# The tokens' scale goes into the halves of x at the end of k, and five evictions lose it

## The chip, the cores and the metric

The kernel runs on one core of a Trainium2 chip. A core has TensorE (PE in the profile, with its weight loads shown apart as PEld), VectorE (DVE), ScalarE (ACT), GpSimd (POOL) and SyncE (SP), which issues nearly all DMAs here. The engines run side by side, each through its own list of instructions, and wait for one another by semaphores. The metric is the time of one execution on the device in microseconds (us), the median of several runs.

## What is computed

Two transformer-like blocks follow each other on 256 tokens of width 1024. The change is in the first one, in how it uses its normalised input `h`:

```python
def first_block(x, ...):
    h = rms_norm(x, norm_w[layer])              # y = x * rsqrt(mean(x*x) + EPS), times norm_w
    proj = h @ w_in[layer].astype(f32)          # 1024 -> all widths
    u_s, z_s, q, k, v, z_a, r_s, r_a = jnp.split(proj, offsets, axis=-1)
    y_s = s5_branch(u_s, ...)                   # state-space branch
    y_s = (y_s * jax.nn.silu(z_s)) @ w_ssm_out[layer].astype(f32)
    q = rms_norm(q...); k = rms_norm(k...)      # per head, then rotary embedding
    y_a = dilated_attention(q, k, v)
    y_a = (y_a * jax.nn.silu(z_a)) @ w_attn_out[layer].astype(f32)
    m = jax.nn.sigmoid(r_s) * y_s + jax.nn.sigmoid(r_a) * y_a
    x = (x.astype(f32) + m @ w_o[layer].astype(f32)).astype(x.dtype)
```

The second block (a gated recurrence, a differential attention, and 32 experts of which each token uses two) is not touched.

## The kernel before

**Scale after the product.** `norm_w` belongs to a column of `h`, the factor `rsqrt(mean)` to a token. The kernel multiplies x by `norm_w` alone (`raw`, L1093), keeps the result as `hr` (f32, 8 pieces of 128 rows by 256 tokens), and starts on the products with `w_in` before the token's factor is known. The factor exists in two forms: `self.rstd`, one number for each partition when tokens lie on partitions, and `self.rows`, all 256 factors in a row on every partition. Each eviction of a product from PSUM multiplies by one of the two.

**Products.** The first block's products come in the order u, k, v, q, za, ra, zs, rs, glu, ao, so, wo. For u and k (`WHOLE`) the f32 operands are multiplied whole (`dense`, L453). For all others both operands are split into a rounded high half on ACT and a low half, the difference, on DVE (`split`, L597), and three products are summed: `dense` again (L453), or `dense_wide` (L477) for v and q. The halves of x are `hT[0]` and `hT[1]`, buffers in the pool R. They are made by `halves(c)`, c = 0 to 3, two of the eight pieces each, from `hr`, and put into a list (`self.mid`) from which `dense` takes a step after every few products of k's last chunk.

**Evictions.** `heads` (k) and `heads2` (q) copy a product out of PSUM on ACT with `rstd`, square it on ACT into a temporary of the small heap E, and add the squares by head on DVE (L1189, L1200). v is copied out on ACT with `rstd`. The gates z and r use `rows`: `scaled` multiplies PSUM by `rows` on DVE, then ACT takes the tanh of the result, and for z (`silu2`) DVE multiplies once more. E holds three temporaries of 128 x 512 at a time, and hands out the one that has been free longest.

**Work beside the products.** The state-space branch runs as a generator (`ssm`, L699), four rounds of 16 groups each: DVE prepares tables, PE makes transposes and small products (L764, L779), DVE turns the states (a scan, L801), and writes them to `hst[0]` and `hst[1]` (L807, L811), which PE reads next (L833, L836). Head normalisation, attention and the splits of the weights (`WR<-WR`, L253 and L272) are woven in as well.

**Order.** The Python code gives an order of the whole. A scheduling layer then places every instruction in its engine's list by what it depends on and by what that layer reckons things take; the lists are fixed in the built program. At run time an engine goes through its list from the front.

**The end.** The experts' weights stream in over the second half. They are issued by SP when buffers come free, so the start of this stream hangs on the products before it.

Of the kernel before, what the change touches and what calls it, by code (L numbers as in the profile page):

```python
# [12 lines left out]
AF = mybir.ActivationFunctionType  # L13
ALU = mybir.AluOpType
# [208 lines left out]
def shaped(ap, shape):  # L223
    if len(shape) == 1:
        return ap
    names = "abcdef"[:len(shape)]
    kw = {n: s for n, s in zip(names[1:], shape[1:])}
    return ap.rearrange(f"p ({' '.join(names)}) -> p {' '.join(names)}", **kw)
# [12 lines left out]
class Kernel:  # L241
# [803 lines left out]
    def first_block(self):  # L1045
# [31 lines left out]
        hr = self.WR.alloc(8, 256, dt=F32)  # L1077
# [29 lines left out]
        hT = []  # L1107

        def halves(c):
            def f():  # L1110
                w = slice(2 * c, 2 * c + 2)
                self.split(hT[0][:, w], hT[1][:, w], hr[:, w])
                if c == 3:
                    hr.free()
            return f
# [36 lines left out]
        for c in range(4):  # L1152
            ev = evac_to(uT)(c)

            def evac(ps, c=c, ev=ev):
                ev(ps)
                nc.sync.dma_start(ud[:, 2 * c:2 * c + 2], uT[:, 2 * c:2 * c + 2])

            if c:
                self.dense("u", hr, None, evac)  # L1160
            else:
                self.dense("u", hr, None, lambda ps, evac=evac: self.mid.extend(
                    [norm, lambda: None, self.token_rows, lambda: evac(ps)]), rows_first=True)
            if c == 1:
                next(tables)
# [17 lines left out]
        def heads(c, raw, sq):  # L1183
            def g(ps):
                self.scaled_tok(raw[:, 2 * c:2 * c + 2].rearrange("p m t d -> p t m d"),
                                ps.rearrange("p t (m d) -> p t m d", m=2))
                t = self.E.alloc(2, 2, 128)
                self.act(t.ap, raw[:, 2 * c:2 * c + 2], AF.Square)
                V.tensor_reduce(out=shaped(sq, (12, 2, 2))[:, 2 * c:2 * c + 2], in_=t.ap.rearrange("p m t (h d) -> p m t h d", d=64),  # L1189
                                axis=AX, op=ALU.add)  # L1190
                t.free()
            return g

        def heads2(c, raw, sq):
            def g(ps, tb):
                w = raw[:, 4 * c:4 * c + 4, tb]
                self.act(w, ps.rearrange("p (m d) -> p m d", m=4), AF.Copy, scale=self.rstd[:, tb:tb + 1])
                t = self.E.alloc(4, 128)
                self.act(t.ap, w, AF.Square)
                V.tensor_reduce(out=shaped(sq, (12, 2, 2))[:, 4 * c:4 * c + 4, tb],  # L1200
                                in_=t.ap.rearrange("p m (h d) -> p m h d", d=64), axis=AX, op=ALU.add)
                t.free()
            return g
# [6 lines left out]

        def silu2(dst, c):
            def g(ps):
                self.silu2(dst[:, 2 * c:2 * c + 2], ps)
            return g

        def tanh_half(dst, c):
            def g(ps):
                self.tanh_half(dst[:, 2 * c:2 * c + 2], ps)
            return g

        def last(which, c):

            if which == WHOLE[-1] and c == 5:
                hT.extend((R.alloc(8, 256), R.alloc(8, 256)))
                self.mid.extend(halves(i) for i in range(4))

        def operand(which):
            return (hr, None) if which in WHOLE else hT

        att = None  # L1230
        for which in ORDER[1:ORDER.index("so")]:
            if which not in WHOLE:
                ssm_side[1] = SIDE[6]
            if which in ("k", "q"):
                raw = big[which]
                raw.ap = shaped(raw.ap, (12, 2, 128))
                sq = self.sq[which]
                if which in WHOLE:
                    for c in range(6):
                        last(which, c)  # L1240
                        self.dense(which, *operand(which), heads(c, raw, sq), token_major=True)
                else:
                    for c in range(3):
                        self.dense_wide(which, *hT, heads2(c, raw, sq))
                preps[which] = self.head_prep(which, raw.ap, sq)
                self.side_add(preps[which], SIDE[1])
                trans[which] = raw
            elif which == "v":
                v = big["v"]
                v.ap = shaped(v.ap, (2, 24, 64))  # L1250
                for c in range(3):
                    def ev(ps, tb, c=c):
                        self.act(v[:, tb, c * 8:c * 8 + 8], ps.rearrange("p (h d) -> p h d", d=64), AF.Copy,
                                 scale=self.rstd[:, tb:tb + 1])
                    self.dense_wide("v", *hT, ev)
            elif which in width:
                g = gate[which] = F.alloc(width[which], 256)
                for c in range(width[which] // 2):
                    self.dense(which, hT[0], hT[1], (silu2 if which[0] == "z" else tanh_half)(g, c))
                if which == LAST_H:  # L1260
                    for b in (*hT, self.rows):
                        b.free()
                    self.rows = None
            elif which == "mask":
                self.amask = F.alloc(1024)
                nc.sync.dma_start(self.amask.ap, I["amask"])
            elif which == "att":
                for n in "qk":
                    self.side_drain(preps[n])
                for n in "qk":  # L1270
                    self.show(n + "T", trans[n].ap.rearrange("p m t d -> p m (t d)"))
                ao = F.alloc(4, 256)
                att = self.attention(trans["q"], trans["k"], v, gate["za"], ao)
                self.side_add(att, SIDE[2])
            elif which == "ssm":
                self.side_drain(ssm)
                for b in self.m3 + self.bbp + [self.bd, self.d0, self.stab] + self.ptab + self.hst + [u2, uT]:
                    b.free()
                self.show("y2", self.g_hi.ap.bitcast(F32))
            elif which == "attend":  # L1280
                self.side_drain(att)
                for b in (trans["q"], trans["k"], v, gate["za"], self.amask):
                    b.free()
                self.show("att", ao.ap)
            elif which == "ao":
                a_hi, a_lo = R.alloc(4, 256), R.alloc(4, 256)
                for hp in range(4):
                    self.split(a_hi[:, hp], a_lo[:, hp], ao[:, hp])
                ao.free()
                ra = gate["ra"]  # L1290
                for c in range(4):
                    def ev(ps, c=c):
                        w = slice(2 * c, 2 * c + 2)
                        self.stt(ra[:, w], ra[:, w], 1.0, ps, ALU.add, ALU.mult)
                    self.dense("ao", a_hi, a_lo, ev, k=4)
                a_hi.free()
                a_lo.free()
            elif which == "glu":
                zs = gate["zs"]
                s_hi, s_lo = R.alloc(8, 256), R.alloc(8, 256)  # L1300
                for c in range(4):
                    def ev(ps, c=c):
                        w = slice(2 * c, 2 * c + 2)
                        t, y = self.E.alloc(2, 256), self.E.alloc(2, 256)
                        self.act(t.ap, ps, AF.Tanh, scale=0.25)
                        self.add(y.ap, self.g_hi[:, w].bitcast(F32), self.g_lo[:, w].bitcast(F32))
                        self.stt(t.ap, t.ap, 1.0, y.ap, ALU.add, ALU.mult)
                        self.mul(t.ap, t.ap, zs[:, w])
                        self.split(s_hi[:, w], s_lo[:, w], t.ap)
                        t.free()  # L1310
                        y.free()
                    self.dense("glu", self.g_hi, self.g_lo, ev)
                self.g_hi.free()
                self.g_lo.free()
                zs.free()
# [1003 lines left out]
```

## Time and profile before

| what | before |
|---|---|
| median of 3 runs (lowest, highest) | 1038.18 us (1036.95, 1039.09) |
| the profiled execution, its own time | 1038.15 us |
| its span, first to last instruction | 1036.4 us |
| busy share PE / DVE / ACT / POOL | 90% / 50% / 34% / 1% |
| mean granted TensorE clock | 0.974 of full speed |

Busy time counts an engine from the start to the end of each instruction. Matmuls overlap each other, so a busy PE has not necessarily a full pace. Times in rows are microseconds from the start of the span; the trace is of one execution.

### The profile page before, as it was taken

Reading aid. Unit: us, or ns where it says so; the run is one execution under the profiler, and the core shown is the slowest. Engines: PE = TensorE matmul, PEld = TensorE weight load, DVE = VectorE, ACT = ScalarE, POOL = GpSimd, SP = SyncE. Lnnn points to the kernel's source line nnn. Section 1 sums busy time; section 2 is a strip of 40 time slices with the busy share of each in tenths; the row PEclk is TensorE's granted clock in tenths of the full one; section 3 lists DMA queues with packets and bytes.
Section 4 is the critical chain, followed back from the end, with each engine's and each line's share of the span. In section 5 each row is a group of like instructions: output and inputs, shape, how many; then the busy total and the mean of one; then the engine's idle time right before and its main releaser. Section 6 shows DMA issues by size and latency. Waiting matters only on the chain.

```text
span 1036.4 us, 16567 instructions
## 1 busy us (share of the span) xinstructions
PE 932.3 (90%) x6723; PEld 644.8 (62%) x6723; DVE 521.0 (50%) x1166; ACT 352.1 (34%) x586; POOL 11.6 (1%) x39
## 2 busy tenths in 40 slices
PE   9999999999999999999999999877868787776875
PEld 6877788998999988888999844221313132131312
DVE  8998988887767778596768521110101010010101
ACT  3237567565564456554654311000000000000000
POOL 2000000000000000000000000000000000000000
PEclk9999999999999999998999999989999898998989
DMA  7754454555447765652569899999999999999996
GB/s 253 221 171 140 145 163 144 169 180 177 149 129 239 229 216 164 197 181 89 184 197 333 328 391 421 421 421 421 421 421 421 421 421 421 421 420 421 421 417 255
DMA packets 61459, 294.24 MB, mean 284 GB/s; under 512 B 10944, under 2 KB 13376, under 8 KB 37824
## 3 DMA queue, kind: packets, MB, share of 16 engines
q1 hardware_dynamic: 61376, 293.11, 75.5%
q8 instruction: 55, 0.90, 0.4%
q14 instruction: 28, 0.23, 0.1%
HBM read 290.98 MB, written 2.10 MB: 283 GB/s over the span
## 4 chain that ended last, share of the span: by engine, by line
PE 54%; DMA 37%; DVE 6%; ACT 2%; issue 1%; POOL 0%; SPq 0%; DVEq 0%; ACTq 0%
PE d L453 27%; DMA heap<-in_w_dram 23%; PE d L477 12%; DMA WR<-in_w_dram 12%; DVE heap L253 3%; PE h L1982 2%; DMA WR<-in_w_last_dram 2%; DVE WR L253 1%; ACT heap L272 1%; PE d L502 1%; PE s L925 1%; PE r L2014 1%; PE o L959 1%; PE s L944 1%; PE d L1804 1%
## 5 line engine op out<-in xcount | busy, mean ns | idle before, releaser
L453 PE MATMUL d<-R,WR 128*128 128x256 f32 x1920 | 240.5, 285 | 0.4 <-DVE WR L253 0.3
L453 PEld LDWEIGHTS d<-R,WR 128*128 128x128 f32 x1920 | 232.8, 192 | 5.2 <-issue 2.6
L1982 PE MATMUL h<-heap 128*32 128x512 f32 x1024 | 179.3, 675 | 61.0 <-DMA heap<-in_w_dram 60.1
L253 DVE TENSOR_TENSOR WR<-WR,WR 128x1024 fp32r<-128x1024 f32 x140 | 171.1, 1223 | 72.4 <-PE d L453 20.7
L272 ACT ACTIVATE WR<-WR 128x1024 fp32r<-128x1024 f32 x140 | 148.2, 1058 | 126.3 <-PE d L453 77.3
L1982 PEld LDWEIGHTS h<-heap 128*32 128x32 f32 x1024 | 40.4, 121 | 185.5 <-DMA heap<-in_w_dram 110.0
L477 PE MATMUL d<-WR,R 128*128 128x512 f32 x624 | 149.5, 396 | 1.9 <-DVE WR L253 1.0
L477 PEld LDWEIGHTS d<-WR,R 128*128 128x128 f32 x624 | 116.1, 189 | 27.7 <-ACT heap L272 1.7
L253 DVE TENSOR_TENSOR heap<-heap 128x512 f32<-128x512 f32 (+7 forms) x250 | 109.4, 493 | 1.1 <-ACT heap L272 0.4
L272 ACT ACTIVATE heap<-heap 128x512 f32<-128x512 f32 (+5 forms) x133 | 68.8, 531 | 60.6 <-DVE heap L253 28.5
L2014 PE MATMUL r<-WR,heap 128*32 128x512 f32 (+1 forms) x288 | 79.3, 550 | 10.8 <-DMA WR<-in_w_dram 9.9
L269 DVE SCALAR_TENSOR_TENSOR WR<-r,ring,WR 128x512 fp32r<-128x512 f32 (+1 forms) x18 | 12.4, 692 | 135.4 <-ACT WR L272 135.4
L2014 PE MATMUL r<-R,heap 128*32 128x512 f32 (+1 forms) x288 | 69.8, 551 | 9.0 <-ACT heap L272 4.8
L453 PE MATMUL d<-WR,WR 128*128 128x256 f32 x320 | 73.1, 388 | 1.1 <-ACT heap L272 1.1
L453 PEld LDWEIGHTS d<-WR,WR 128*128 128x128 f32 x320 | 61.5, 194 | 11.5 <-ACT heap L272 2.6
L253 DVE TENSOR_TENSOR heap<-heap,h 128x512 f32<-128x512 f32 x8 | 5.5, 687 | 117.3 <-PE h L1982 117.2
L2014 PEld LDWEIGHTS r<-WR,heap 128*32 128x32 f32 x288 | 19.0, 109 | 56.5 <-DMA WR<-in_w_dram 27.0
L272 ACT ACTIVATE WR<-r,ring 128x512 fp32r<-128x512 f32 (+1 forms) x18 | 11.5, 640 | 123.9 <-PE r L2014 112.2
L272 ACT ACTIVATE heap<-h,ring 128x512 f32<-128x512 f32 x8 | 5.5, 687 | 141.3 <-PE h L1982 119.7
L269 DVE SCALAR_TENSOR_TENSOR heap<-heap,h 128x512 f32<-128x512 f32 x8 | 5.5, 687 | 90.3 <-ACT heap L272 90.3
L2014 PEld LDWEIGHTS r<-R,heap 128*32 128x32 f32 x288 | 14.6, 109 | 36.0 <-issue 15.5
L272 ACT ACTIVATE heap<-r 128x512 f32<-128x512 f32 x8 | 4.8, 597 | 82.4 <-PE r L1997 82.4
(211 smaller groups left out, 798.6 us busy)
## 6 DMA issues: line engine op xcount, KB each, us to landing
heap<-in_w_dram SPq DMA_DIRECT2D x128, 1024.0 KB, 19.8
WR<-in_w_in_dram SPq DMA_DIRECT2D x114, 512.0 KB, 4.0
R<-in_w_dram SPq DMA_DIRECT2D x28, 1024.0 KB, 19.8
WR<-in_w_dram SPq DMA_DIRECT2D x28, 1024.0 KB, 19.8
WR<-in_w_wo_dram SPq DMA_DIRECT2D x16, 512.0 KB, 5.9
WR<-in_w_glu_dram SPq DMA_DIRECT2D x8, 512.0 KB, 4.1
WR<-in_w_so_dram SPq DMA_DIRECT2D x8, 512.0 KB, 4.6
R<-in_w_last_dram SPq DMA_DIRECT2D x8, 512.0 KB, 12.6
```

The costliest lines, as they stand in the source:

```text
L253: (eng or self.V).tensor_tensor(out=out, in0=a, in1=b, op=op)
L269: self.V.scalar_tensor_tensor(out=out, in0=a, scalar=s, in1=b, op0=op0, op1=op1)
L272: self.A.activation(out, a, func, **kw)
L453: self.PE.matmul(ps[:, j], lhsT, rhs, start=h == 0 and i == 0 and n == 0, stop=h == k - 4 and kk == 3 and n == len(terms) - 1, skip_group_ ...
L477: self.PE.matmul(ps[tb], x[:, h + kk, sl], w[:, kk], start=h == 0 and kk == 0 and n == 0, stop=h == 6 and kk == 1 and n == 2)
L502: self.PE.matmul(ps[c][:, j], lhsT, rhs, start=h == 0 and i == 0 and n == 0, stop=h == 4 and kk == 3 and n == 2, skip_group_check=True)
L925: PE.matmul(ps[hh][:, cols], qT[r, q, qs], kT[r, q, k], start=True, stop=True)
L944: PE.transpose(pt[:, kb], s[:, kb * 128:(kb + 1) * 128], self.ident)
L959: PE.matmul(po[hp][r, qb], v[:, tb, g * 8 + hp * 2 + hh], ts_[hh][:, kb], start=kb == 0, stop=kb == 3)
L1804: PE.matmul(ps, x[:, 4 * h + kk, tb * 128:tb * 128 + 128], ws[h][w][:, kk], start=h == 0 and kk == 0 and n == 0, stop=h == 1 and kk == 3 a ...
L1982: PE.matmul(ph[sl[g]], xg[:, kk, sl[g]], w(name, kk // 4, g)[:, kk % 4], start=kk == 0, stop=kk == 7)
L2014: PE.matmul(pys[c][sl[g]], hT[:, kk, sl[g]], rhs, start=kk == 0, stop=kk == 3)
```

## The change

The scale moves from the evictions to the operand. `halves(c)` first multiplies its two pieces of `hr` by `rows` on DVE, into a temporary of E, and splits that instead of `hr`. So `hT` holds the halves of the finished `h`, and every product that reads `hT` comes out scaled. The evictions of q, v, za, ra, zs and rs lose the factor: the ACT copies of q and v keep their place without `rstd`; for the four gates the DVE multiplication falls away, ACT takes the tanh from PSUM directly, and the last DVE operation of `silu2` reads PSUM too. u and k keep their scaling, since they multiply `hr`. The second block keeps its own.

```diff
         def halves(c):
             def f():
                 w = slice(2 * c, 2 * c + 2)
-                self.split(hT[0][:, w], hT[1][:, w], hr[:, w])
+                t = self.E.alloc(2, 256)
+                self.scaled(t.ap, hr[:, w])
+                self.split(hT[0][:, w], hT[1][:, w], t.ap)
+                t.free()
                 if c == 3:
                     hr.free()
...
-                self.act(w, ps.rearrange("p (m d) -> p m d", m=4), AF.Copy, scale=self.rstd[:, tb:tb + 1])
+                self.act(w, ps.rearrange("p (m d) -> p m d", m=4), AF.Copy)
...
         def silu2(dst, c):
             def g(ps):
-                self.silu2(dst[:, 2 * c:2 * c + 2], ps)
+                t = self.E.alloc(2, 256)
+                self.act(t.ap, ps, AF.Tanh, scale=0.5)
+                self.stt(dst[:, 2 * c:2 * c + 2], t.ap, 1.0, ps, ALU.add, ALU.mult)
+                t.free()
...
         def tanh_half(dst, c):
             def g(ps):
-                self.tanh_half(dst[:, 2 * c:2 * c + 2], ps)
+                self.act(dst[:, 2 * c:2 * c + 2], ps, AF.Tanh, scale=0.5)
```

The order in PE's list stays the same up to the attention's transposes, but DVE's and ACT's lists change. The first place is ACT's list at the start of the program, where x arrives (`WR<-heap,prm` is a piece of `hr`, `heap<-heap` the square for the mean, `R<-WR` the high half of x):

```order
 L272 ACTIVATE ring<-ones 128x1
 L272 ACTIVATE WR_64<-heap,prm 128x256
 L272 ACTIVATE heap<-heap 128x512
-L272 ACTIVATE R_61<-WR_64 128x512
 L272 ACTIVATE WR_64<-heap,prm 128x256
 L272 ACTIVATE heap<-heap 128x512
-L272 ACTIVATE R_61<-WR_64 128x512
```

All four high halves, and on DVE the four subtractions for the low ones, leave the first 14 us. They come back in the second place, during the products of k. On ACT, the rows ahead are the copies of the first round's block matrix from PSUM (`heap<-s`) and eight small copies for the second round (`64x8x16`), the rows behind k's next eviction (`d,rstd`):

```order
 L272 ACTIVATE heap<-s 32x8x32 x4
 L272 ACTIVATE heap<-heap 64x8x16 x8
+L272 ACTIVATE R_61<-heap 128x512 x2
 L272 ACTIVATE heap<-d,rstd_210 128x2x128 x2
 L272 ACTIVATE heap<-heap 128x8x63
 L272 ACTIVATE heap<-heap 128x512
 L272 ACTIVATE WR_67<-WR_63 128x1024
-L272 ACTIVATE WR_851<-WR_97 128x1024
+L272 ACTIVATE R_61<-heap 128x512
```

Two of the four high halves now stand behind those eight copies, one behind the next split of weights, and the fourth further down. The third place is DVE's list at the same time. Before, the sums of k's squares (L1189) are followed by the second round's preparation and by the first round's states, which DVE takes from PSUM (`s_515`):

```order
L253 TENSOR_TENSOR heap<-heap 128x512 x13
L1189 TENSOR_REDUCE heap<-heap 128x8
L253 TENSOR_TENSOR heap<-heap 128x512 x2
L253 TENSOR_TENSOR heap<-heap 128x2x32 x2
L266 TENSOR_SCALAR heap<-heap 128x2x32
L1189 TENSOR_REDUCE heap<-heap 128x8
L253 TENSOR_TENSOR heap<-heap 128x512 x2
L253 TENSOR_TENSOR heap<-s_515,heap 128x2x4x64 x2
```

Now the same line stands three lines lower in the file (L1192), and two whole splits stand between the third sum and the first round's states:

```order
L253 TENSOR_TENSOR heap<-heap 128x512 x12
L1192 TENSOR_REDUCE heap<-heap 128x8 x2
L253 TENSOR_TENSOR heap<-WR_64,heap 128x512
L253 TENSOR_TENSOR R_62<-heap,R_61 128x512
L253 TENSOR_TENSOR heap<-WR_64,heap 128x512
L253 TENSOR_TENSOR R_62<-heap,R_61 128x512
L253 TENSOR_TENSOR heap<-heap 128x512 x2
L253 TENSOR_TENSOR heap<-s_515,heap 128x2x4x64 x2
```

Each split is a multiplication by `rows` into the temporary, and a subtraction that needs ACT's high half of it. The two are `halves(0)` and `halves(3)`. Both were given the same piece of E (that of the third k chunk's squares), so the second multiplication overwrites what the first subtraction reads, and comes after it. `halves(1)` and `halves(2)` stand 20 to 40 instructions further down. Behind these rows DVE's list is the same up to the writing of `hst[0]`.

## Rows read from the trace of the kernel before

**Rows 1.** Cores: span and mean granted clock.

```profile
core 0: 1036.4 us, clock 0.974
```

**Rows 2.** Stretches: length, busy time by engine, granted clock, DMA share, GB/s.

```profile
core 0: us, PE busy (x) PEld busy (x) DVE busy (x) ACT busy (x) POOL busy (x), PEclk, DMA share, GB/s
60.00:92.50 32.50, 29.63 (x385) 25.31 (x377) 27.16 (x44) 16.48 (x36) 0.00 (x0) 1.00 0.39 129
92.50:122.00 29.50, 28.69 (x275) 23.02 (x273) 29.46 (x55) 20.27 (x38) 0.00 (x0) 1.00 0.50 149
...
177.00:328.00 151.00, 150.15 (x1473) 142.83 (x1471) 120.10 (x248) 86.35 (x137) 1.08 (x2) 1.00 0.51 167
328.00:545.00 217.00, 215.85 (x1506) 195.10 (x1505) 160.31 (x296) 118.58 (x178) 0.53 (x1) 0.98 0.58 186
545.00:606.00 61.00, 60.26 (x428) 52.11 (x427) 37.23 (x88) 21.91 (x39) 3.38 (x15) 1.00 0.90 337
606.00:1036.00 430.00, 335.40 (x1934) 113.32 (x1932) 45.93 (x132) 32.13 (x64) 0.00 (x0) 0.95 0.99 410
```

**Rows 3.** Chain that ended last, where it passes from PE to DMA: start, length, what.

```profile
642.89 2.81 PE h L1982 x24
...
645.71 20.95 DMA WR<-in_w_dram
```

**Rows 4.** Waits of PE, 0 to 400 us: us in total, times, longest.

```profile
PE s L833 <- DVE heap L253: 1.8, 1, 1.8
...
PE s L779 <- ACT heap L272: 1.1, 2, 0.6
PE d L477 <- ACT heap L272: 0.9, 1, 0.9
```

**Rows 5.** Timeline of PE, 58 to 82 us: start, length, idle time before.

```profile
61.33 9.33 PE L453 MATMUL d<-WR,WR 128*128 128x256 f32 x42
72.45 0.43 PE L833 MATMUL s<-heap 128*32 128x64 f32 x16 [1.79 <-DVE heap L253]
72.81 2.86 PE L453 MATMUL d<-WR,WR 128*128 128x256 f32 x12
```

**Rows 6.** Timeline of DVE, 56 to 76 us.

```profile
60.75 0.69 DVE L1189 TENSOR_REDUCE heap<-heap 128x8 f32<-128x512 f32 x1 [2.41 <-ACT heap L272]
61.35 1.41 DVE L253 TENSOR_TENSOR heap<-heap 128x512 f32<-128x512 f32 x2
62.68 1.28 DVE L253 TENSOR_TENSOR heap<-s,heap 128x512 f32<-128x512 f32 x2
```

**Rows 7.** Timeline of ACT, 58.5 to 73 us.

```profile
62.16 2.31 ACT L272 ACTIVATE heap<-heap 64x128 f32<-64x128 f32 x8
68.54 0.84 ACT L272 ACTIVATE heap<-d,rstd 128x256 f32<-128x256 f32 x2 [4.06 <-PE d L453]
```

**Rows 8.** Halves of x, 5 to 15 us: ns least/median/most, first and last start.

```profile
L272 ACT ACTIVATE R<-WR x4: 614/614/614, 6.2 to 12.2; 128x512 fp32r<-128x512 f32 x4
L253 DVE TENSOR_TENSOR R<-WR,R x4: 683/684/687, 7.4 to 13.5; 128x512 fp32r<-128x512 f32 x4
```

**Rows 9.** Groups by form, 177 to 332 us, a split of activations: busy, mean ns, idle before.

```profile
L253 DVE TENSOR_TENSOR R<-heap,R 128x512 fp32r<-128x512 f32 x4 | 2.8, 692 | 2.8 <-ACT R L272 2.8
...
L272 ACT ACTIVATE R<-heap 128x512 fp32r<-128x512 f32 x4 | 2.5, 631 | 2.7 <-DVE heap L253 2.7
```

**Rows 10.** Groups by form, 177 to 332 us, the gates' multiplications by `rows`.

```profile
L253 DVE TENSOR_TENSOR heap<-d,heap 128x512 f32<-128x512 f32 x14 | 9.6, 684 | 0.0
```

**Rows 11.** Timeline of PE, 855 to 885 us, an expert's products around a wait.

```profile
856.77 3.63 PE L1982 MATMUL h<-heap 128*32 128x512 f32 x30
...
865.92 6.01 PE L1982 MATMUL h<-heap 128*32 128x512 f32 x30 [0.73 <-DMA heap<-in_w_dram]
```

**Rows 12.** Stretches behind that wait, columns as in Rows 2.

```profile
866.00:870.00 4.00, 4.00 (x20) 0.92 (x24) 0.00 (x0) 0.00 (x0) 0.00 (x0) 0.50 1.01 420
870.00:873.00 3.00, 1.93 (x14) 0.44 (x6) 0.46 (x1) 0.69 (x1) 0.00 (x0) 0.92 1.02 426
```

More of the change, by code (lines that the diff above doesn't have):

```diff
@@ L1252, in ev @@
                     def ev(ps, tb, c=c):
-                        self.act(v[:, tb, c * 8:c * 8 + 8], ps.rearrange("p (h d) -> p h d", d=64), AF.Copy,
-                                 scale=self.rstd[:, tb:tb + 1])
+                        self.act(v[:, tb, c * 8:c * 8 + 8], ps.rearrange("p (h d) -> p h d", d=64), AF.Copy)
                     self.dense_wide("v", *hT, ev)
```

## Prediction

> **What bounds the kernel now.** I read the cores first: one core, span 1036.4 us, clock 0.974 [rows 1]. The profiled execution took 1038.15 us, 1.75 us more than its span, and the median of the runs is 1038.18, so sums made against this execution need no correction. Next the stretches [rows 2]. PE is full wherever the change acts: it idles 2.87 us between 60 and 92.5 (the end of k), 0.81 in the first part of v up to 122, 0.85 in the gates and ra, rs (177 to 328), 1.15 in the rest of the block. DVE is full only between 92.5 and 122 (29.46 of 29.50 us); in the gates it has 31 us to spare. From 606 us on DMA is full (0.99) and PE is not: there the weights' stream sets the time. The chain that ended last [rows 3] says what the stream's start hangs on: back to 645.71 us it is DMA, and ahead of that it is PE. So whatever PE loses in the first block starts the stream later, and the end moves by as much; whatever PE wins is won to the end. The waits of PE [rows 4] then give the places where the first block loses time at all. The longest is 1.8 us, at the first reading of `hst[0]` (L833), for DVE.
>
> The timeline of PE shows that place [rows 5]: k's last products run from 61.33 to 70.66, PE idles 1.79, reads `hst[0]` at 72.45, and behind that stand k's last twelve products. DVE's timeline shows what makes it late [rows 6]: DVE idles 2.41 us up to 60.75 for ACT's square of k's third chunk, sums it, and goes on at 61.35 with the turning of the states, the scans and the writing of `hst[0]`, up to PE's read at 72.45. Each microsecond put into DVE's list between the two is therefore a microsecond of PE's wait.
>
> **What is taken from the start: 0.** Four copies on ACT (614 ns each, 2.5 us) and four subtractions on DVE (684 ns each, 2.7 us) leave the first 14 us [rows 8]. What DVE wins there it would spend in the 2.41 us of idling at 60.75 [rows 6], since that wait ends with ACT's square, and the square with PE's products, in an unchanged order. If that cover were gone, all of PE's 1.79 us [rows 5] would be the gain; so 0, bounds -1.8 and 0.
>
> **What is put in at the end of k: +6.4.** `halves(0)` and `halves(3)` stand in DVE's list right behind the sum of 60.75 and ahead of the states. I follow them with durations of rows: 684 ns for a multiplication by `rows` (that from PSUM [rows 10]; the new one reads SBUF), 631 for the copy and 692 for the subtraction of a split of activations [rows 9].
>
> - The first multiplication starts at 61.35, where the first TENSOR_TENSOR of [rows 6] starts now, and ends at 62.03.
> - ACT's high half of it stands behind the eight copies that run from 62.16 to 64.47 [rows 7]: 64.47 to 65.10. ACT idles 4.06 us behind them, so nothing else stands there.
> - The first subtraction therefore runs from 65.10 to 65.79; DVE waits 3.07 us for it, with everything behind it ready.
> - The second multiplication writes the piece that this subtraction reads: 65.79 to 66.47. Copy to 67.10, subtraction to 67.79.
> - The states' first operation, now at 61.35, starts at 67.79: 6.44 us later.
>
> Lower bound: were the eight copies of no account (ACT's list another at run time than I read it), the six operations one behind another are 4.0 us. Upper bound: 6.4 and some 0.3 for handoffs between engines, 6.7. I take 6.4, since each step of it has its row. PE's wait at L833 becomes 1.79 + 6.44 = 8.2 us, 70.66 to 78.9. Queued behind it on PE are k's last twelve products, and with them its eviction, all of v and the rest; nothing else can run there.
>
> [...]
>
> **The clock after the stall: +1.6.** No stretch of the dense part shows PE after 8 us of idling. [...] Lower bound 0 (the clock stays; behind PE's 1.79 us of idling the twelve f32 products ran at their usual pace [rows 5]). [...]
>
> **The rest of the halves, in v: +0.5.** `halves(1)` falls among operations behind the reading of `hst[0]`, where DVE has idled for some of its 5.3 us (27.16 busy of 32.5 [rows 2], 2.41 of them ahead of that [rows 6]), and trails a PE that is later itself: 0. One split's multiplication and subtraction (0.68 + 0.69 = 1.4 us) come ahead of the next round's states in the stretch where DVE is full [rows 2]. PE's idle there is 0.8 us, so DVE sets the pace for a part only. Bounds 0 and 1.4, taken 0.5.
>
> **What the evictions lose: -0.4.** The copies of q and v on ACT keep their instruction without its scale: 0. In the gates, ra and rs 14 multiplications go, 9.6 us of DVE [rows 10]. DVE had 31 us of slack there and PE idled 0.85 us out of 151 [rows 2], so 0.85 is the most that can come back; the waits of PE for the two other places of the block are 1.1 and 0.9 us in all [rows 4], and not for these multiplications. Bounds -0.85 and 0, taken -0.4. The tanh, now from PSUM, and the last operation of `silu2` are one instruction each as before; a bank of PSUM is held longer by the tanh less the multiplication, well under 1 us, where evictions come some 10.8 us apart (14 in 151 us [rows 2, 10]).
>
> **Sum.** 6.4 + 1.6 + 0.5 - 0.4 = +8.1 us: 1038.15 + 8.1 = 1046.2 us. With all lower bounds 4.0 + 0 + 0 - 1.8 - 0.85 = +1.4 (1039.5), with all upper ones 6.7 + 2.4 + 1.4 + 0 = +10.5 (1048.7).
>
> **Rivals.** A measurement of this kernel tells a time from no change from about 0.2% on, 2.1 us.
>
> *The clock does not fall.* Same stall, but PE goes on at full pace: 1038.15 + 6.4 + 0.5 - 0.4 = 1044.7. For it: 1.79 us of idling did nothing [rows 5]. Against it: [rows 12]. Chance 0.20. [...]
>
> *The stream swallows it.* If the weights' transfers were behind for their own sake (DMA share 0.90 already in 545 to 606 [rows 2]), a later PE would only use up the lead with which buffers come free, and the time stays at 1038.2. Against it: the chain passes to PE at 645.7 with 2.81 us of PE's own products ahead of it [rows 3]. Chance 0.07.
>
> *Faster.* The work taken from the start lets DVE prepare the second round earlier; the scheduling also moved two operations away from between the second and third sum. If ACT's copies that the split awaits come ahead of the eight (that is, if these eight are held up by something late), and the third sum itself comes more than 4 us earlier, `hst[0]` is not later, and the waits of [rows 4] and the gates' 0.85 us are gained: 1038.15 - 1.8 - 0.85 - 0.6 = 1034.9. It decides only if the square of the third chunk is not paced by PE; that ACT stands idle for 4.06 us until the products of the next eviction are done [rows 7] says that it is. Chance 0.04.
>
> *Worse.* The stall as above, and the full DVE of the v stretch takes its 1.4 us whole and a second stall of the same length as the upper clock term follows: 1048.7 + 2.4 = 1051. For it: DVE has 0.04 us of slack in 92.5 to 122 [rows 2]. Against it: PE is later by then too, which gives DVE its time. Chance 0.08.
>
> **How the numbers follow.** The forecast has the remaining 0.61, and 1046.2 is its time; its own range, with one term at a time at its bounds, is 1044 to 1048.5. The range for 8 in 10 takes in the rival without the clock's fall and the lower bound of the stall (1046.2 - 2.4 - 1.6 = 1042.2), and the sum of the upper bounds: 1041.5 to 1049.5. It leaves out "no change", "faster" and most of "worse", 0.19 together. Faster by over 0.2%: 0.04. Within: 0.07. Slower: 0.89.
>
> **What would show it.** The wait of PE at L833 for DVE grows from 1.8 to about 8 us. Ahead of the first subtraction into R after the third sum, DVE waits about 3 us for ACT. The granted clock falls to 0.5 for some us between 75 and 85. In 177 to 328 us, shifted by 8, the 14 multiplications of [rows 10] are gone, and PE's idle stays under 1 us. The chain passes from PE to DMA at about 654. I am wrong if the wait at L833 is under 5 us, if the stretches behind k are shifted by less than 6, or if the chain from PE no longer leads to the end.

## The result and the profile after

The changed kernel takes 1046.12 us (1044.68 to 1046.86, four runs) against 1038.63 for the kernel before, timed beside it. The ratio is 1.0072, with a 95% interval from 1.0059 to 1.0085: slower by 7.5 us. The forecast was 8.1 us more. (The title counts five evictions that lose the scale; the change has six, those of q, v, za, ra, zs and rs.)

The cores' view of the profiled execution gives a longer span and a lower mean clock than [rows 1]:

```profile
core 0: 1044.0 us, clock 0.965
```

The waits of PE from 0 to 400 us answer to [rows 4]. The one at L833 has grown from 1.8 to 8.3 us:

```profile
PE s L833 <- DVE heap L253: 8.3, 1, 8.3
```

The timeline of PE shows the same place as [rows 5]:

```profile
61.64 9.33 PE L453 MATMUL d<-WR,WR 128*128 128x256 f32 x42
79.30 0.65 PE L833 MATMUL s<-heap 128*32 128x64 f32 x16 [8.32 <-DVE heap L253]
79.88 4.54 PE L453 MATMUL d<-WR,WR 128*128 128x256 f32 x12
84.35 0.99 PE L833 MATMUL s<-heap 128*32 128x64 f32 x56
```

PE comes here 0.3 us late, idles 8.32 us, and then needs 4.54 us for the twelve rows that took 2.86. Up to the second start of L833 it now takes 5.05 us from the first (84.35 - 79.30). Before, that was 3.14 us (75.59 - 72.45 in [rows 5]), with this row of the trace before:

```profile
75.59 0.99 PE L833 MATMUL s<-heap 128*32 128x64 f32 x56
```

The stretches after (columns as in [rows 2]) show the granted clock while these rows run: 0.62 on average. It is 0.50 from 79.3 to 83 us, 0.84 in the next microsecond, and 1.00 again from 84 us on.

```profile
80.00:84.40 4.40, 4.40 (x16) 3.36 (x20) 4.40 (x8) 0.63 (x1) 0.00 (x0) 0.62 0.12 20
84.00:88.00 4.00, 4.00 (x124) 3.34 (x124) 2.35 (x4) 1.41 (x4) 0.00 (x0) 1.00 0.35 126
```

What is late is read from DVE's timeline, at the place of [rows 6]:

```profile
61.07 0.69 DVE L1192 TENSOR_REDUCE heap<-heap 128x8 f32<-128x512 f32 x1 [4.44 <-ACT heap L272]
61.79 0.69 DVE L253 TENSOR_TENSOR heap<-WR,heap 128x512 f32<-128x512 f32 x1
65.48 0.69 DVE L253 TENSOR_TENSOR R<-heap,R 128x512 fp32r<-128x512 f32 x1 [3.00 <-ACT R L272]
66.21 0.69 DVE L253 TENSOR_TENSOR heap<-WR,heap 128x512 f32<-128x512 f32 x1
67.60 0.69 DVE L253 TENSOR_TENSOR R<-heap,R 128x512 fp32r<-128x512 f32 x1 [0.69 <-ACT R L272]
68.21 1.41 DVE L253 TENSOR_TENSOR heap<-heap 128x512 f32<-128x512 f32 x2
```

The third sum (61.07) is where it was. Behind it stand the two splits, each a multiplication and a subtraction, and DVE waits 3.00 and 0.69 us for ACT's high halves. The states' first operation starts at 68.21 instead of 61.35. ACT's timeline, at the place of [rows 7], tells why the first wait is the longer one: the high half stands behind the eight small copies.

```profile
62.48 2.31 ACT L272 ACTIVATE heap<-heap 64x128 f32<-64x128 f32 x8
64.82 0.63 ACT L272 ACTIVATE R<-heap 128x512 fp32r<-128x512 f32 x1
66.94 0.63 ACT L272 ACTIVATE R<-heap 128x512 fp32r<-128x512 f32 x1 [1.48 <-DVE heap L253]
```

The multiplication was done at 62.48 (61.79 + 0.69). ACT's copy of its result started 2.3 us later, when the eight were through.

The way to the end is followed by pieces of the chains that ended last. Before:

```profile
122.12 13.91 PE d L477 x60
...
328.22 29.03 PE d L453 x240
...
540.49 22.79 PE d L453 x190
...
606.62 10.44 PE h L1982 x96
...
1016.52 10.07 DMA WR<-in_w_last_dram
```

After:

```profile
130.89 13.90 PE d L477 x60
...
336.24 29.03 PE d L453 x240
...
548.43 22.78 PE d L453 x190
...
619.06 15.55 DMA heap<-in_w_dram
...
1024.22 10.07 DMA WR<-in_w_last_dram
```

PE is 8.77 us late in v, 8.02 behind the gates, 7.94 at 548, and the last transfer is 7.70 late: the stall goes through to the end but for what the gates give back and 0.3 us ahead of the experts. One sign of the forecast did not come: the chain passes from PE to DMA at 619.06, behind the first experts' products, and not at about 654. The products are still what leads there. The place is not a fixed one: in the evictions alone, below, the chain passes at 625, and with the halves early at 610.

The gates' stretch, shifted by 8 us, against the 150.15 us of PE and 120.10 of DVE in [rows 2]:

```profile
185.00:336.00 151.00, 150.95 (x1479) 143.72 (x1477) 112.78 (x235) 84.84 (x138) 1.08 (x2) 1.00 0.51 167
```

PE idles 0.05 us there, 0.80 less. The multiplications of [rows 10] are gone from the groups; DVE reads a product's tile (`d`) there in only eight operations, the six last ones of `silu2` and two that stood there before.

### The profile page after: what moved, and what is told of

It is laid out like the page before. It is cut to its first block, busy times and chain, and to the rows that moved or that the text cites. A ratio compares the mean times of both kernels' runs of the same rounds, so it can differ in the third digit from the quotient of the medians.

```text
span 1044.0 us, 16553 instructions
## 1 busy us (share of the span) xinstructions
PE 936.3 (90%) x6723; PEld 646.4 (62%) x6723; DVE 515.6 (49%) x1156; ACT 349.8 (34%) x586; POOL 11.9 (1%) x39
## 4 chain that ended last, share of the span: by engine, by line
PE 51%; DMA 40%; DVE 5%; ACT 1%; issue 1%; SPq 0%; POOL 0%; DVEq 0%; ACTq 0%
PE d L453 28%; DMA heap<-in_w_dram 26%; PE d L477 12%; DMA WR<-in_w_dram 11%; DVE heap L253 3%; DMA WR<-in_w_last_dram 2%; PE d L502 1%; PE s L925 1%; DVE WR L253 1%; ACT heap L272 1%; PE o L959 1%; PE s L944 1%; PE s L836 1%; DMA WR<-in_w_in_dram 1%; PE h L1987 1%
## 5 line engine op out<-in xcount | busy, mean ns | idle before, releaser
L1987 PE MATMUL h<-heap 128*32 128x512 f32 x1024 | 181.7, 680 | 58.5 <-DMA heap<-in_w_dram 57.5
L1987 PEld LDWEIGHTS h<-heap 128*32 128x32 f32 x1024 | 41.5, 121 | 184.3 <-DMA heap<-in_w_dram 109.6
L272 ACT ACTIVATE heap<-heap 128x512 f32<-128x512 f32 (+7 forms) x119 | 59.9, 519 | 52.9 <-DVE heap L269 15.8
L272 ACT ACTIVATE heap<-s 128x512 f32<-128x512 f32 (+3 forms) x59 | 27.5, 488 | 16.1 <-PE s L1447 7.6
```

Of the source, the lines that this page charges most:

```text
L272: self.A.activation(out, a, func, **kw)
L1987: PE.matmul(ph[sl[g]], xg[:, kk, sl[g]], w(name, kk // 4, g)[:, kk % 4], start=kk == 0, stop=kk == 7)
```

## The experiments

Theory: two splits stand ahead of the first round's states in DVE's list, and PE waits for these; then the clock falls. Rivals: the price is DVE's added work, wherever it stands; or the evictions from PSUM cost a part. Each ratio below is to runs of the kernel before on the same chip. The first four experiments ran on one chip and the other four on another, so times of the two groups are compared by their ratios. Where an edit adds lines to the file, the line numbers in its rows are a few higher (L833 is L837 or L840).

**The halves alone.** In the kernel before, `halves` as in the change, evictions untouched.

> The kernel before with scaled halves alone: the six evictions keep their factor too, so these products carry the tokens' scale twice. Theory (the two splits ahead of the states stall PE, the evictions give a little back): the wait at L833 is 8.3 us as in the changed kernel, the clock falls behind it, and without the gates' 0.9 us the time is 1046.1 + 0.9 = 1047.0. Rival (a part of the loss comes from the evictions, tanh and last operation now on PSUM): the time is clearly below 1046.

1046.76 us, ratio 1.0078 (1.0064 to 1.0091). The wait at L833 is 8.3 us, the twelve rows take 4.61 us:

```profile
78.99 0.66 PE L833 MATMUL s<-heap 128*32 128x64 f32 x16 [8.32 <-DVE heap L253]
79.58 4.61 PE L453 MATMUL d<-WR,WR 128*128 128x256 f32 x12
```

The whole loss is in the halves; the evictions cost nothing.

**The evictions alone.** In the changed kernel:

```diff
-                t = self.E.alloc(2, 256)
-                self.scaled(t.ap, hr[:, w])
-                self.split(hT[0][:, w], hT[1][:, w], t.ap)
-                t.free()
+                self.split(hT[0][:, w], hT[1][:, w], hr[:, w])
```

> The changed kernel with the halves taken from hr as before, so the products of hT are left unscaled. Theory: no stall at L833 beyond the 1.8 us of before, the 14 multiplications of the gates gone, PE's idle there gone: 1038.6 - 0.9 = 1037.7. Rival (evictions from PSUM hold banks and cost): 1039 or more. Second rival (DVE's freed 9.6 us matter more than PE's idle says): below 1036.

1037.05 us, ratio 0.9983 (0.9973 to 0.9993): a gain, and a small one. PE's wait at L833 is 1.8 us, as before. The stretch of the gates shows where it is. PE's idle of 0.85 us [rows 2] is down to 0.13, although DVE has 31 us of slack there before and 38 us here:

```profile
177.00:328.00 151.00, 150.87 (x1478) 143.61 (x1478) 113.20 (x235) 84.74 (x138) 1.08 (x2) 1.00 0.51 169
```

**The high half on DVE.** This takes the waits for ACT away and adds work to DVE:

```diff
-                self.split(hT[0][:, w], hT[1][:, w], t.ap)
+                V.tensor_copy(hT[0][:, w], t.ap)
+                self.sub(hT[1][:, w], t.ap, hT[0][:, w].bitcast(F32))
```

> The changed kernel with the halves' high part copied by DVE in place of ACT. Theory (DVE's waiting for ACT is over half of the stall): six operations one behind another, at most 4.1 us ahead of the states in place of 6.5, wait at L833 about 5.9 us, time 1046.1 - 2.4 = 1043.7, less if a copy is shorter than 0.69 us. Rival (the price is the work added to DVE, the waits are of no account): eight more copies or two more ahead of the states, 1.3 us more: 1047.4.

1043.26 us, ratio 1.0045 (1.0032 to 1.0059). DVE's timeline has the six operations one behind another, without a wait:

```profile
61.15 0.69 DVE L253 TENSOR_TENSOR heap<-WR,heap 128x512 f32<-128x512 f32 x1
61.88 0.43 DVE L1114 CAST R<-heap 128x512 fp32r<-128x512 f32 x1
62.34 0.69 DVE L253 TENSOR_TENSOR R<-heap,R 128x512 fp32r<-128x512 f32 x1
...
64.86 1.41 DVE L253 TENSOR_TENSOR heap<-heap 128x512 f32<-128x512 f32 x2
```

The states start 3.7 us behind the first multiplication instead of 6.4 (68.21 - 61.79), and the wait at L833 is 5.6 us:

```profile
75.95 0.65 PE L833 MATMUL s<-heap 128*32 128x64 f32 x16 [5.60 <-DVE heap L253]
76.53 4.29 PE L453 MATMUL d<-WR,WR 128*128 128x256 f32 x12
```

More work on DVE, and a faster kernel than the changed one, by 2.8 us as the ratios have it (1.0072 and 1.0045). In the changed kernel the two waits for ACT are 3.69 of the 6.42 us ahead of the states (3.00 + 0.69); with two copies of 0.43 us in their place the 6.42 fall to 3.71 (64.86 - 61.15).

**One split ahead.** Temporaries of two following splits are held together, so they get different pieces of E; that moves the second split behind `hst[0]`:

```diff
-        hT = []
+        hT, held = [], []
...
+                held.append(t)
                 self.scaled(t.ap, hr[:, w])
                 self.split(hT[0][:, w], hT[1][:, w], t.ap)
-                t.free()
+                if c % 2:
+                    while held:
+                        held.pop().free()
```

> The changed kernel with the temporaries of two following splits held together, so that they lie in different pieces of E; DVE's list then has one split ahead of the first round's states, the other behind hst[0]. Theory: the first subtraction still waits for ACT's copy behind the eight, and ends at 66.2; the states start 4.4 us late instead of 6.5, the wait at L833 is about 6.2 us, time 1046.1 - 2.1 = 1044.0. Rival (what counts is DVE's work, half of it gone): the stall falls by half to 3.2, 1042.8. Rival (not the splits ahead of the states): no change, 1046.1.

1044.20 us, ratio 1.0054 (1.0040 to 1.0068), the wait at L833 6.2 us:

```profile
76.59 0.66 PE L833 MATMUL s<-heap 128*32 128x64 f32 x16 [6.21 <-DVE heap L253]
77.17 4.11 PE L453 MATMUL d<-WR,WR 128*128 128x256 f32 x12
```

Half of the work is gone from the place and 2.1 us of the 6.5, as the theory has it: the first subtraction, alone, waits as long as before.

```profile
61.19 0.69 DVE L253 TENSOR_TENSOR heap<-WR,heap 128x512 f32<-128x512 f32 x1
64.89 0.69 DVE L253 TENSOR_TENSOR R<-heap,R 128x512 fp32r<-128x512 f32 x1 [3.00 <-ACT R L272]
65.50 1.41 DVE L253 TENSOR_TENSOR heap<-heap 128x512 f32<-128x512 f32 x2
```

**The halves behind the states.** The same work, at another place of DVE's and ACT's lists (`turned` holds the instruction that writes `hst[1]` of the first round; `issue_after` queues DVE's operations behind it, and ACT's copies follow):

```diff
-            self.add(self.hst[1][:, :, z], t1[:, :, a], t2[:, :, a])
+            self.turned.append(V.tensor_tensor(out=self.hst[1][:, :, z], in0=t1[:, :, a], in1=t2[:, :, a], op=ALU.add).ins)
...
-                t = self.E.alloc(2, 256)
-                self.scaled(t.ap, hr[:, w])
-                self.split(hT[0][:, w], hT[1][:, w], t.ap)
-                t.free()
+                with self.tc.issue_after(self.turned[0]):
+                    t = self.E.alloc(2, 256)
+                    self.scaled(t.ap, hr[:, w])
+                    self.split(hT[0][:, w], hT[1][:, w], t.ap)
+                    t.free()
```

> The changed kernel with all operations of the halves queued behind the writing of hst[1] of the first round. Theory (the splits cost because they stand ahead of the states, not for their work): the wait at L833 is at most the 1.8 us of before, the clock stays, and the time is that of the evictions alone, 1037.1, plus what of 5.5 us of DVE's work doesn't fit in the 2.9 us that DVE idles from 61 to 92 us: 1037 to 1039.5. Rival (the work itself is the price, wherever it stands): DVE is full in v, so all of 5.5 us returns there, 1042 or more.

1038.53 us, ratio 1.0007 (0.9996 to 1.0019). The wait is 1.78 us again, and the twelve rows take 2.86 us, as before:

```profile
72.28 0.43 PE L833 MATMUL s<-heap 128*32 128x64 f32 x16 [1.78 <-DVE heap L253]
72.64 2.86 PE L453 MATMUL d<-WR,WR 128*128 128x256 f32 x12
75.42 0.99 PE L833 MATMUL s<-heap 128*32 128x64 f32 x56
```

The loss is gone with the place alone: of 0.72% the ratio has 0.07% left, which is not told from nothing. The time does not show the gates' gain, but the chain does:

```profile
122.83 13.90 PE d L477 x60
...
328.18 29.03 PE d L453 x240
```

From 122.83 to 328.18 PE takes 205.35 us, 0.75 less than the 206.10 before (328.22 - 122.12): that is the gain, and PE's idle time in 177 to 328 is 0.06 us. From the second start of L833 (75.42) to 122.83 it takes 47.41 us, 0.88 more than before (122.12 - 75.59 = 46.53): that is the halves' work in v, where DVE is full, and it takes the gain back.

**The halves early.** In k's first chunk instead of its last:

```diff
-            if which == WHOLE[-1] and c == 5:
+            if which == WHOLE[-1] and c == 0:
...
+            if which == WHOLE[-1] and c == 5:
+                self.mid.extend([lambda: None] * 3 + [hr.free])
```

> The changed kernel with the halves put into k's first chunk in place of its last; hr is given back where it was. Theory: DVE idles 4.4 us ahead of the third sum in the changed kernel; 5.5 us of splits ahead of it delay that sum by 1.1 us at most, and hst[0] with it: wait at L833 up to 2.9 us, no fall of the clock, 1037.1 to 1038.3. Rival (DVE is full from 20 to 40 us, so u's evictions and the first transposes come late): PE waits at L764 or in u, 1040 or more.

1037.81 us, ratio 1.0001 (0.9992 to 1.0009). The wait at L833 is 2.1 us; DVE, which idles 4.44 us ahead of the third sum in the changed kernel, is busy up to it here: the row of the sum has no idle time ahead of it. The work fits into that idle time. The sum comes 0.35 us later than before (60.75), and the wait is 0.34 longer.

```profile
61.10 0.67 DVE L1190 TENSOR_REDUCE heap<-heap 128x8 f32<-128x512 f32 x1
...
72.77 0.43 PE L833 MATMUL s<-heap 128*32 128x64 f32 x16 [2.13 <-DVE heap L253]
```

**The third sum late as well.** On top of the halves behind the states, the third sum is queued behind the writing of `hst[0]`.

> The kernel of halves_behind, with the sum of k's third squares queued behind the writing of hst[0]. Theory: DVE no longer waits 4.4 us for ACT's square, the next bound is the states' products of PE (L779, done at 61.4 us in the kernel before, where the states start at 62.68): hst[0] 1.3 us earlier, wait at L833 about 0.5 us, time 1.3 us under halves_behind. Rival (the piece of E that the squares hold comes free later and stops the fourth chunk's eviction or a split): no gain or a loss.

1037.60 us, ratio 0.9997 (0.9987 to 1.0007): not told apart from the kernel before, and the expectation missed. The wait at L833 fell only to 1.4 us, where 0.5 was expected. I had taken the two operations ahead of the states for ready; DVE's timeline says they wait for the products of L779 too, so that DVE only changed what it waits for:

```profile
61.30 1.42 DVE L253 TENSOR_TENSOR heap<-heap 128x512 f32<-128x512 f32 x2 [4.67 <-PE s L779]
...
72.40 0.43 PE L837 MATMUL s<-heap 128*32 128x64 f32 x16 [1.41 <-DVE heap L807]
```

**The clock.** Six idle products, whose result nothing uses (twelve rows, since each product has two), on PE ahead of L833. They can start when the first scan is done:

```diff
+FILL = 6
...
+            if B == 0:
+                pd = self.psum("s", 256)
+                for i in range(FILL):
+                    PE.matmul(pd, self.ident, fl(g1.ap)[:, :256], start=i == 0, stop=i == FILL - 1)
+                g1.free()
```

> The changed kernel with six idle products of 128x256 (f32) on PE, which read the result of the first scan, so that PE works for the last 4 us ahead of L833; their sum is used nowhere. PE's order moves with them: five products of k's fifth chunk stand behind L833's first eight, in place of six, and eleven come later. Theory (the twelve products behind the wait are slow because the clock fell): the idle products take the low clock, and the five behind L833 run at 0.24 us a piece of two, 2.3 us for ten rows, with a granted clock of 1.0. Rival (they are slow for another reason, for instance their operands): 0.38 us each as in the changed kernel, 3.8 us for ten rows.

The profile of this single run, with its order shifted as expected:

```profile
74.77 4.37 PE L831 MATMUL s<-heap,cst 128*128 128x256 f32 x12 [6.17 <-DVE heap L802]
79.07 0.46 PE L840 MATMUL s<-heap 128*32 128x64 f32 x16
79.46 2.43 PE L454 MATMUL d<-WR,WR 128*128 128x256 f32 x10
```

Its stretches, with the granted clock:

```profile
75.00:79.00 4.00, 4.00 (x12) 3.07 (x12) 3.97 (x7) 1.93 (x3) 0.00 (x0) 0.64 0.00 0
79.30:84.00 4.70, 4.54 (x88) 3.73 (x80) 4.70 (x9) 0.63 (x1) 0.00 (x0) 1.00 0.02 3
```

Now the idle products are the slow ones, 0.36 us a row at a clock of 0.64, and those of k behind L833 run at 0.24 a row and 1.00. What is slow in this trace is what comes first after the wait of 6.17 us. The whole kernel gains nothing by it (1046.77, one run): ten rows of k that ran ahead of the wait in the changed kernel come behind it here, where 32 rows and not 42 stand ahead of the wait.

## Why the prediction was right

- **The path to the end.** That a later PE is a later end held: 8.02 us behind the gates, 7.70 at the last transfer. The weights' stream swallowed nothing: PE's run of L1982 that starts at 606.62 before starts at 614.28 after (L1987), 7.66 later. The 0.3 us went ahead of that, on PE itself: 0.08 up to 548 us, and 0.26 in eight products (L1768, now L1773) that took 1.08 us before and 0.82 after. The expected place of the change from PE to DMA in the chain, 654, was wrong (619.06); no term of the sum hung on it.
- **The stall, +6.4.** Measured +6.53 (8.32 - 1.79). DVE's wait for ACT was forecast at 3.07 us and is 3.00; the two-part structure, waits and serial splits, is shown by the copies on DVE and by the single split ahead. DVE kept the order of its list here, as the forecast's steps have it: the states, though ready, started 6.42 us behind the first multiplication (68.21 - 61.79), after the waiting splits, and with the splits queued behind them the loss was gone. DVE's 2.41 us ahead of 60.75 [rows 6] do not show this order: in the run with the third sum late, the operations behind that sum wait for L779 until 61.30, 0.8 us behind L779's start. Before the change L779 starts at 60.16, so by an estimate (60.16 + 0.8) they were ready at 61.0, when that wait was over. The 3.00 us in the changed kernel do show the order: they run from 62.48 to 65.48, and L779 was done at 61.71. The 0.3 us for handoffs in the upper bound was the author's estimate; around the second copy they took 0.04 us (66.90 to 66.94) and 0.03 us (67.57 to 67.60).
- **The clock, +1.6.** Measured +1.91: from the first to the second start of L833 it is 3.14 us before and 5.05 after. Shorter waits cost nearly as much: the twelve rows take 4.29 us after 5.6 us of idling and 4.11 after 6.2, against 2.86. No run shows the 1.6 us, or the 2.4 of its upper bound, as a cost of one wait: they were the author's estimates, 2.4 from an expert's products (6.01 - 3.63 us [rows 11]) and 1.6 as two thirds of it. Those products stand behind several waits and not one: PE idled 0.54, 1.45 and 0.73 us between 860 and 866, and the clock was at 0.50 from 864 us on, before the last of these. They were a rough stand-in, and the two thirds a guess that came near.
- **The rest in v, +0.5.** Measured 0.0: PE is 8.76 us late at L833's second start and 8.77 at 130.89. DVE's full stretch was no bound once PE was late: with PE in time (the halves behind the states) the work cost 0.88 us there. This term was mis-sized, within its bounds.
- **The evictions, -0.4.** Measured -0.75 in the chain and -0.80 in the stretch, nearly the bound of -0.85: the multiplications were on the way of PE's small waits after all. Mis-sized too.
- **The start, 0.** The lead was swallowed as forecast: DVE's idling ahead of the third sum went from 2.41 to 4.44 us. PE came to the place 0.31 us late, at 61.64. With the same order of PE's list up to there it came between 61.02 and 61.66 in the other runs' traces, with differing waits for the first weights, so this is put down to the execution.

Sum: 0.31 + 6.53 + 1.91 + 0 - 0.75 = 8.0, less the 0.3 us at the end 7.7; the spans differ by 7.6. The forecast of 8.1 was so near because v's term was 0.5 and the gates' 0.35 too high, and the start, the stall and the clock 0.31, 0.13 and 0.31 too low: 0.85 us one way and 0.75 the other. The mechanism was right and its largest term well sized; that the total came within 0.6 us is in part luck. One name was wrong: the twelve rows behind L833 belong to k's fifth chunk of six, not to its last. No number hung on it.

What remains open: by the ratios (0.9983 and 1.0007) the halves behind the states take 0.24% or 2.5 us more than the evictions alone. The work in v accounts for 0.9 us of it in the profiled executions; the rest lies within the two intervals or was not located. No version beat the kernel before by more than its interval, but for the evictions alone, which leave the factor out.

## What to carry to other kernels

The same 5.5 us of an engine's work cost nothing measurable or 8 us here, by its place in that engine's list: look at what stands behind it, ready, and at whom the work itself waits for. A round trip to a second engine in the middle of a list cost what stood ahead in the second engine's list as well: for the same copy of 0.63 us DVE waited 3.00 us the first time and 0.69 the second. 0.43 us more on the first engine was cheaper than those 3 us. A term for the clock belongs into the sum where a full PE comes to a wait like these: behind 5.6 to 8.3 us of idling the twelve rows took 1.25 to 1.75 us more.

## What the runs showed of the hardware

DVE's copy with one input (f32 to fp32r, from SBUF) took 0.43 us for 128x512 where its operation with two inputs took 0.69 and ACT's copy 0.63. Behind waits of 5.6, 6.2 and 8.3 us the twelve rows took 1.4, 1.3 and 1.7 us more (the granted clock was 0.62 on average behind the last), and single waits of 1.8 and 2.1 us in an otherwise full PE cost none: the twelve rows took 2.86 us behind both.
